# Recurrence gates as four 64x64 tiles, recurrence products moved off GpSimd, and the next layer's modulation moved into the recurrence's stage

## The chip, the cores and the metric

The kernel runs on one core of one Trainium2 chip. The metric is the device time of one execution in microseconds; the times of the kernel before are the median of three runs. In the profile PE is the matrix engine, PEld its weight loads, DVE the vector engine, ACT the scalar engine, POOL is GpSimd, and SP is the queue from which every DMA of this kernel is issued.

## The reference, cut to what matters

The program is a trunk of two layers over 512 latent and 256 context tokens of width 1024. Each layer normalises the tokens, scales and shifts them by a modulation that is computed from the conditioning vectors, multiplies them by one wide input projection, and feeds three branches: a gated delta rule (GDN), a gated linear recurrence (RG-LRU) and neighbourhood attention. Each branch has a SiLU gate path and a branch projection, the three are merged under sigmoid gates, and one output projection with a modulated residual ends the layer.

```python
shift, scale, gate = split(silu(c) @ w_mod[l] + b_mod[l], 3)      # also for c_ctx
h = rms_norm(x, g_pre[l]) * (1 + scale) + shift

def rglru(x, wa, ba, wx, bx, lam, h0):       # one direction; two are run
    r = sigmoid(block_diag_linear(x, wa, ba))     # 8 blocks of 64 x 64
    i = sigmoid(block_diag_linear(x, wx, bx))
    a = exp(-8 * r * softplus(-lam))
    b = sqrt(1 - a * a) * (i * x)
    h[t] = a[t] * h[t - 1] + b[t]
merged = g0 * (ya @ w_branch[0]) + g1 * (yb @ w_branch[1]) + g2 * (yc @ w_branch[2])
x = x + gate * rms_norm(merged @ w_out, g_post[l])
```

The second layer has no context output, so most of its work covers only the 512 latent tokens.

## The kernel before

Every fp32 matrix is split into two fp16 parts (`whi`, `wlo`), and a projection is three fp16 products: high by high, high by the low part of the data, low by high. Weights come from HBM in raw tiles of 512 KB (256 KB for a branch projection) through a ring of three slots (`raw_t`, L305); ACT makes the high part, DVE the low part.

The order of the instructions is written by a planner (`Flow`, L50). Generators ask it for times (`fl.until`), it keeps estimated clocks for every engine, and it emits the instructions in the order of its own clock; each engine then runs them strictly in that order. A layer's main generator walks through `schedule(l)` (L208): the GDN and attention inputs; the first merge stage `gb(2)` (eight pairs of a gate projection `g` and a branch projection `b` for attention), beside which the second half of the GDN's chunk chain still runs; the projections `za`; the recurrence's stage with the tokens zb 0, xb 0, xb 1, zb 1, xb 2, zb 2, xb 3, zb 3; then `gb(0)` for the GDN branch, two `g` and two `b` of branch 1, the token `out`, the rest of `gb(1)` and the output projection. The first branch-1 projection waits until all recurrence groups have ended (`yield core`, L1653).

**The recurrence** (`rg_core`, L886) works on four groups of 128 channels, each with two of the 64-wide blocks. Per group: the convolution; `xh` and `xl`, the fp16 parts of its result; the weights `lw`, for each direction and gate a 128x128 matrix with two 64x64 blocks on the diagonal and zeros beside them; then `yield before` (L899), which holds the group until the group before it has written its output. For each direction and each of the two gates (`tr`, `ti`) there are two segments (512 and 256 columns) of three products into one PSUM bank, evacuated by ACT with a tanh. ACT computes `aa` and the second tanh, DVE squares `aa`, ACT takes the square root of `zz`, GpSimd multiplies `ix` by `zz` (L934), DVE runs four scans, GpSimd adds the two directions (L953), DVE multiplies by the SiLU gate and ACT and DVE write the fp16 output `yb`.

**The modulation** of the next layer (`modulation`, L519; `mod_rows`, L475) is computed in two halves of eight steps. A step takes a 512 KB tile `wm` and issues eight products `pm` of 128x32 tiles in four column strips. After the eighth, ACT copies the row out of PSUM and eight small products `pmt` turn it into columns. In layer 0 the main generator takes one step of it at each token of `gb(2)`, through `wload` (L534) and the ring of raw slots, one tile ahead; what is left is drained when `gb(2)` ends (L1658). The third part of the modulation, the gate row (`gate_rows`, L540), has its own two `wm` buffers in the recurrence's pool, is taken step by step in the recurrence's stage and `gb(0)`, and ends with a row addition on DVE, loads of `selg` and `gp` through the ring, and the broadcast products `pg`:

```python
V.tensor_tensor(row, pm, row, OP.add)
selg = raw_t([P, 2, 2, P], "selg")
nc.sync.dma_start(selg, A["selg"])
yield
for n in range(2):
    for s in range(1 if l == DEPTH - 1 else 2):
        mm(pg, selg[:, n, s, :], row, start=True, stop=True)
```

Of the kernel before, what the change touches and what calls it, by code (L numbers as in the profile page):

```python
# [14 lines left out]
OP = mybir.AluOpType  # L15
# [220 lines left out]
def build(tc, A, out):  # L236
# [282 lines left out]
    def modulation(l, out_, halves, load, rowt):  # L519

        def fin(hf):
            def f(pm):
                row = rowt()
                S.activation(row, pm, AF.Copy)
                fl.drop(pm)
                yield
                mod_cols(l, out_, row, 4 * hf, 4)
            return f

        mod_tiles(l, out_)  # L530
        for hf in halves:
            yield from mod_rows(l, hf, fin(hf), load)

    def wload(l, part, k):  # L534
        raw = raw_t([P, 2, 2, 256], "wm")
        nc.sync.dma_start(raw, A["w_mod"][l, part, k])
        fl.fetched(raw, True)
        return raw

    def gate_rows(l, pp, wp_, out_, rowt):  # L540

        row = rowt()
        nc.sync.dma_start(row, A["b_gate"][l])

        def fin(pm):
            V.tensor_tensor(row, pm, row, OP.add)
            fl.drop(pm)
            gg = pp.tile([P, 2, D], F32, name="gg")
            selg = raw_t([P, 2, 2, P], "selg")
            nc.sync.dma_start(selg, A["selg"])  # L550
            fl.fetched(selg, True)
            g = A["g_post"]
            gp = raw_t([P, D], "gp")
            nc.sync.dma_start(gp, bass.AP(tensor=g.tensor, offset=g.offset + l * D, ap=[[0, P], [1, D]]))
            fl.fetched(gp, True)
# [3 lines that stand above are left out]
                    pg = pst(f"pg{l}_{n}_{s}", [P, 512])  # L559
                    mm(pg, selg[:, n, s, :], row, start=True, stop=True)  # L560
                    V.scalar_tensor_tensor(gg[:, s, n * 512:(n + 1) * 512], pg, 1.0 / SW,
                                           gp[:, n * 512:(n + 1) * 512], op0=OP.mult, op1=OP.mult)
            fl.drop(selg, gp)
            fl.used[selg.name] = fl.now
            out_["gg"] = gg

        def load(l, part, i):
            t = wp_.tile([P, 2, 2, 256], F32, tag="wm", name="wm", bufs=2)
            nc.sync.dma_start(t, A["w_mod"][l, part, i])
            fl.fetched(t)  # L570
            return t

        yield from mod_rows(l, 2, fin, load, 2)
# [189 lines left out]
    def layer(l, mod, first):  # L763
# [116 lines left out]
        def load_lw(j):  # L880
            t = rp.tile([P, 4, P], F32, tag="lw", name="lw", bufs=2)
            nc.sync.dma_start(t, A["lru_w"][l, j])
            fl.fetched(t)
            return t

        def rg_core(pp, yb, j, lwr, b, before):  # L886
# [5 lines left out]
            yield fl.until(xh)  # L892
            V.tensor_tensor(xl, xb[:, :NT + GAP], xh, OP.subtract)
            yield fl.until(lwr)
            lw = [pp.tile([P, 4, P], F16, tag=f"lw{i}", name=f"lw{i}", bufs=2) for i in range(2)]
            S.activation(lw[0], lwr, AF.Copy, scale=SW)
            yield fl.until(lw[0])
            V.scalar_tensor_tensor(lw[1], lwr, SW, lw[0], op0=OP.mult, op1=OP.subtract)
            yield before  # L899
            yield fl.until(xl, *lw)  # L900
            aa = pp.tile([P, 2, NT], F32, tag="aa", name="aa")
# [3 lines left out]
            for d in range(2):  # L905
                tr = pp.tile([P, NT], F32, tag="tr", name="tr")
                ti = pp.tile([P, NT], F32, tag="ti", name="ti")
                for w_, dst in ((0, tr), (1, ti)):
                    wi = (d * 2 + w_) * 4 + j
                    for a, b, xo in xsegs:  # L910
                        yield from fl.room()
                        p = pst("lru", [P, b - a])
                        for n, (i, x_) in enumerate(((0, xh), (0, xl), (1, xh))):
                            mm(p, lw[i][:, d * 2 + w_, :], x_[:, xo:xo + b - a], start=n == 0, stop=n == 2)
                        S.activation(dst[:, a:b], p, AF.Tanh, scale=0.5 / SW, bias=lrb[:, wi:wi + 1])
                        yield 0.0
                if d == 1:
# [9 lines left out]
                yield fl.until(aa)  # L927
                V.tensor_tensor(zz[:, d, :], aa[:, d, :], aa[:, d, :], OP.mult)
                yield fl.until(tr, zz)
# [3 lines left out]
            yield fl.until(zz)  # L933
            G.tensor_tensor(ix, ix, zz, OP.mult)  # L934
            yield fl.until(ix)
            hs = []
            for d in range(2):
                hh = pp.tile([P, NT], F32, tag=("tr", "ti")[d], name="hh")
                if d == 0:
# [9 lines left out]
                hs.append(hh)  # L949
                yield fl.until(hh)  # L950
            z = zview(yb, j)
            yield lambda: ("zb", j) in gates and gates["zb", j].done
            G.tensor_tensor(hs[0][:, :ntok], hs[0][:, :ntok], hs[1][:, :ntok], OP.add)  # L953
            yield fl.until(hs[0])
            V.tensor_tensor(hs[0][:, :ntok], hs[0][:, :ntok], z[:, :ntok], OP.mult)
            yield fl.until(hs[0])
            yield from put_y(yb, j, hs[0], 0.5 * UN)
            yield fl.until(yb)

        xfree = []  # L960
        BLK = (0, 8, 24, 32)
# [639 lines left out]

        merged, gated = {}, {}
        nxt, read, turned = {}, set(), []
        with ExitStack() as layer_:
# [11 lines left out]
            for tkn in schedule(l):  # L1616
                kind = tkn[0]
                if kind == "merge":
# [6 lines left out]
                    for half in halves:  # L1625
                        for u in range(2):
                            outs.append(fl.spawn(gdn_out(mp, half, ya, u, ended(*outs)), 4))
                    side = iter(()) if last else modulation(l + 1, nxt, (0, 1), wload, rowt)
                    continue
# [34 lines left out]
                if kind == "xb" and tkn[1]:  # L1664
                    lwr = load_lw(tkn[1])
                if kind in ("xb", "zb") and rp is not None:
                    if need is not None:
                        yield fl.until(need)
                    need = next(side, None)
# [5 lines left out]
                if opening and kind == "xb":  # L1675
# [7 lines left out]
                    rp = rgs.enter_context(tc.tile_pool(name=f"rg{l}", bufs=1, side="right", reuse_waits="tile"))  # L1683
                    side = gate_rows(l, ggp, rp, nxt, rowt)
                if kind == "a":
# [115 lines left out]
def _layout(i):  # L1801
# [27 lines left out]
    o["lru_b"] = np.stack([a["lru_ba"], a["lru_bx"]], 2).reshape(L, 16, P).transpose(0, 2, 1)  # L1829
    lw = np.zeros((L, P, 2, 2, 4, P), np.float32)  # L1830
    for k, name in enumerate(("lru_wa", "lru_wx")):
        v = a[name].reshape(L, 2, 4, 2, 64, 64)
        for b in range(2):
            lw[:, 64 * b:64 * b + 64, :, k, :, 64 * b:64 * b + 64] = v[:, :, :, b].transpose(0, 3, 1, 2, 4)
    o["lru_w"] = lw.reshape(L, P, 4, 4, P).transpose(0, 3, 1, 2, 4)
    pool = np.concatenate([a["rpb"].reshape(L, NH, -1), np.full((L, NH, 1), NEG, np.float32),
# [34 lines left out]
```

## Time and profile before

| what | value |
|---|---|
| time, median of 3 runs | 1683.18 us (1683.06 to 1683.78) |
| the profiled execution's own time | 1683.76 us |
| its span, first to last instruction | 1682.0 us |
| mean granted clock of the matrix engine | 0.993 |
| busy: PE, DVE, ACT, GpSimd | 1616.8, 1206.9, 877.9, 279.5 us |

A busy PE counts from a product's start to its modelled end, and products overlap: one of 512 fp16 columns is shown with 379 ns although the next starts long before that. So two products' starts tell the cost, not their durations. Layer 0's first merge stage lies from 417 to about 608 us, its recurrence's stage from 608 to 692, `gb(0)` to 807; in layer 1 the recurrence's stage begins at about 1427 and `gb(0)` ends at about 1577.

### The profile page before, as it was taken

To read this page: it belongs to the slowest core of one execution; us is meant where nothing else is said; L and a number is where in the kernel's file an instruction comes from. 1 tells how busy PE (TensorE), PEld (TensorE's weight loads), DVE (VectorE), ACT (ScalarE), POOL (GpSimd) and SP (SyncE) were. 2 spreads that over 40 slices of the span, in tenths; PEclk is the share of its full clock that TensorE was granted. 3 is DMA by queue.
4 is the path that set the end of the run, shared out by engine and by line. 5 is a ranking of instruction groups with operands and counts; after the bars stand their busy time and mean duration, and the time that the engine had idled before them with its cause. 6 is when DMAs were issued, how large, how long until landed. Compare 5 with 4: busy or idle time off the path is not lost. (4 is left out here: it accounts for less than half of the span.)

```text
span 1682.0 us, 30788 instructions
## 1 busy us (share of the span) xinstructions
PE 1616.8 (96%) x11652; PEld 1027.5 (61%) x11652; DVE 1206.9 (72%) x2896; ACT 877.9 (52%) x2107; POOL 279.5 (17%) x423
## 2 busy tenths in 40 slices
PE   5999999999999999999999999999999999999997
PEld 3666877766667655565664565677766666544443
DVE  5678888775878737775445666989777998688654
ACT  4446665545555426662344544766455666656531
POOL 3003120001322001132120001222003220013310
PEclk9999999999999999999999999999999999999999
DMA  9211011121222333223242122110121112532432
GB/s 369 68 63 58 27 45 45 39 65 36 89 70 70 107 120 125 75 65 101 87 158 80 60 64 64 57 33 28 56 70 50 57 39 76 170 113 88 142 122 76
DMA packets 48389, 139.83 MB, mean 83 GB/s; under 512 B 8048, under 2 KB 8688, under 8 KB 48240
## 3 DMA queue, kind: packets, MB, share of 16 engines
q1 hardware_dynamic: 48240, 137.86, 25.4%
q8 instruction: 91, 1.49, 0.4%
q14 instruction: 58, 0.48, 0.1%
HBM read 133.64 MB, written 4.19 MB: 82 GB/s over the span
## 5 line engine op out<-in xcount | busy, mean ns | idle before, releaser
L264 PEld LDWEIGHTS <-whi_g 128*128 128x128 f16 x1152 | 108.3, 98 | 77.3 <-issue 1.2
L199 DVE SCALAR_TENSOR_TENSOR wlo_g<-raw,whi_g 128x512 f16<-128x512 f32 x96 | 90.7, 985 | 23.8 <-ACT whi_g L199 23.8
L264 PE MATMUL py<-wo,mg 128*128 128x512 f16 x480 | 104.7, 379 | 1.5 <-ACT mt L199 1.5
L264 PEld LDWEIGHTS <-whi_a 128*128 128x128 f16 x736 | 69.1, 98 | 46.2 <-issue 2.7
L264 PE MATMUL 1_g<-h,whi_g 128*128 128x512 f16 x384 | 93.7, 379 | 0.0
L199 ACT ACTIVATE X<-px 128x256 f16<-128x256 f32 x169 | 63.0, 383 | 58.2 <-PE px L264 54.7
L264 PE MATMUL 0_g<-h,whi_g 128*128 128x512 f16 x384 | 93.1, 379 | 0.0
L199 DVE SCALAR_TENSOR_TENSOR coa<-cba,cva,coa 128x770 f32<-128x770 f32 (+1 forms) x72 | 70.8, 984 | 17.2 <-ACT coa L199 15.9
L264 PEld LDWEIGHTS <-mg 128*128 128x128 f16 x480 | 47.0, 98 | 57.2 <-issue 1.8
L199 ACT ACTIVATE di<-py 64x128 f16<-64x128 f32 x234 | 62.8, 271 | 33.5 <-PE py L264 14.2
L264 PEld LDWEIGHTS <-whi_b 128*128 128x128 f16 x576 | 53.5, 98 | 41.0 <-issue 3.4
L199 POOL TENSOR_SCALAR_AFFINE_SELECT dec<-dec 128x256 f32<-128x256 f32 x48 | 23.6, 498 | 325.6 <-ACT dec L199 284.5
L264 PEld LDWEIGHTS <-wlo_g 128*128 128x128 f16 x576 | 54.3, 98 | 37.0
L199 POOL MEMSET cba<- 128x2 f32 (+1 forms) x72 | 3.8, 100 | 436.9 <-DVE coa L199 304.4
L199 DVE TENSOR_TENSOR ic<-pp,lmc 128x128 f16<-128x128 f32 x240 | 65.3, 284 | 4.0 <-PE pp L264 1.1
L199 ACT ACTIVATE whi_g<-raw 128x512 f16<-128x512 f32 x96 | 55.1, 626 | 13.3 <-DMA raw<-in_w_in 13.2
L199 POOL TENSOR_TENSOR gm<-trir,gst 128x256 fp32r<-128x256 f32 x96 | 61.6, 667 | 1.2
L264 PEld LDWEIGHTS <-di 128*128 128x128 f16 x480 | 41.2, 98 | 31.0 <-issue 9.6
L199 DVE CAST di<-py 64x128 f16<-64x128 f32 x150 | 43.0, 287 | 23.9 <-ACT di L199 15.9
L199 DVE SCALAR_TENSOR_TENSOR wlo_b<-raw,whi_b 128x512 f16<-128x512 f32 x48 | 38.6, 804 | 21.4 <-ACT whi_b L199 21.4
L264 PE MATMUL pp<-X,ld 128*128 128x64 f16 x480 | 51.8, 192 | 2.3 <-ACT Y L199 0.3
L199 POOL TENSOR_TENSOR mt<-mg,mt 128x768 f32<-128x768 f32 (+1 forms) x16 | 33.1, 2072 | 117.6 <-DVE mt L199 117.6
(657 smaller groups left out, 4401.6 us busy)
## 6 DMA issues: line engine op xcount, KB each, us to landing
raw<-in_w_in SPq DMA_DIRECT2D x128, 512.0 KB, 3.6
wm<-in_w_mod SPq DMA_DIRECT2D x48, 512.0 KB, 4.3
raw<-in_w_branch SPq DMA_DIRECT2D x48, 256.0 KB, 2.6
rwo<-in_w_out SPq DMA_DIRECT2D x16, 512.0 KB, 3.6
xt<-in_xin SPq DMA_DIRECT2D x12, 512.0 KB, 5.0
bias<-in_rpb SPq DMA_DIRECT2D x24, 256.0 KB, 2.9
lw<-in_lru_w SPq DMA_DIRECT2D x8, 256.0 KB, 3.4
x<-xo SPq DMA_DIRECT2D x4, 512.0 KB, 2.9
```

What stands on the lines that cost most here:

```text
L199: return real(*args, **kw)
L264: nc.tensor.matmul(dst, lhsT, rhs, **kw)
```

## The change

- **Gates.** `lw` holds, per direction, four 64x64 blocks: rows 0 to 63 the first gate's, rows 64 to 127 the second gate's, columns by block. Each of the three terms is four products of 64x64 tiles at tile positions (0,0), (0,64), (64,0), (64,64), which write both gates' banks, a bank each. Since each gate needs both blocks in its own row half, `xh` and `xl` get copies with the halves exchanged (`xs0`, `xs1`), made by four DMAs on SP per group. Two banks are asked for at once (`fl.room(2)`).
- **Groups overlap.** Instead of the group before having ended, a group's gates wait for its scans (`scanned`); `tr` and `ti` have two buffers; the wait for the group before stands at the end.
- **Engines.** The square of `aa` goes from DVE to ACT; the product `ix` by `zz` (in two halves) and the sum of the directions go from GpSimd to DVE.
- **Modulation.** `modulation(l + 1)` runs behind the gate row's steps (`aside`), with the gate row's `wm` buffers, two tiles ahead. Steps are taken at the tokens of the recurrence's stage, in layer 0 two per token from zb 1 on (before and after its projection), none at xb 1, and at the tokens of `gb(0)`. The first merge stage has none.

```diff
-    def wload(l, part, k):
-        raw = raw_t([P, 2, 2, 256], "wm")
...
+            yield from mod_rows(l, hf, fin(hf), load, 2)
+    def wload_of(wp_):
+        def load(l, part, i):
+            t = wp_.tile([P, 2, 2, 256], F32, tag="wm", name="wm", bufs=2)
+            nc.sync.dma_start(t, A["w_mod"][l, part, i])
+            fl.fetched(t)
+            return t
+        return load
...
             V.tensor_tensor(xl, xb[:, :NT + GAP], xh, OP.subtract)
+            yield fl.until(xl)
+            xsw = []
+            for i, x_ in enumerate((xh, xl)):
+                xsw.append(pp.tile([P, NT + GAP], F16, tag=f"xs{i}", name=f"xs{i}"))
+                for a in (0, 64):
+                    nc.sync.dma_start(xsw[i][a:a + 64], x_[64 - a:128 - a])
+                fl.ready[xsw[i].name] = fl.now + FETCH + 0.5
...
-            yield before
-            yield fl.until(xl, *lw)
+            yield lambda: len(scanned) >= j
+            yield fl.until(xl, *xsw, *lw)
...
-                for w_, dst in ((0, tr), (1, ti)):
-                    wi = (d * 2 + w_) * 4 + j
-                    for a, b, xo in xsegs:
-                        yield from fl.room()
-                        p = pst("lru", [P, b - a])
-                        for n, (i, x_) in enumerate(((0, xh), (0, xl), (1, xh))):
-                            mm(p, lw[i][:, d * 2 + w_, :], x_[:, xo:xo + b - a], start=n == 0, stop=n == 2)
-                        S.activation(dst[:, a:b], p, AF.Tanh, scale=0.5 / SW, bias=lrb[:, wi:wi + 1])
-                        yield 0.0
+                for a, b, xo in xsegs:
+                    yield from fl.room(2)
+                    ps = [pst(f"lru{w_}", [P, b - a]) for w_ in range(2)]
+                    cols = slice(xo, xo + b - a)
+                    for n, (i, x_) in enumerate(((0, 0), (0, 1), (1, 0))):
+                        for w_, h0 in ((0, 0), (0, 1), (1, 0), (1, 1)):
+                            r_, c_ = slice(64 * w_, 64 * w_ + 64), slice(64 * h0, 64 * h0 + 64)
+                            nc.tensor.matmul(ps[w_][c_], lw[i][r_, d, c_], ((xh, xl) if h0 == w_ else xsw)[x_][r_, cols],
+                                             start=n == 0, stop=n == 2, tile_position=(64 * w_, 64 * h0))
+                        fl.product(ps[0], (b - a) / 2400.0 + 0.03)
+                    fl.product(ps[1], 0.0)
+                    for w_, dst in ((0, tr), (1, ti)):
+                        wi = (d * 2 + w_) * 4 + j
+                        S.activation(dst[:, a:b], ps[w_], AF.Tanh, scale=0.5 / SW, bias=lrb[:, wi:wi + 1])
+                    yield 0.0
...
-                V.tensor_tensor(zz[:, d, :], aa[:, d, :], aa[:, d, :], OP.mult)
+                S.activation(zz[:, d, :], aa[:, d, :], AF.Square)
...
-            G.tensor_tensor(ix, ix, zz, OP.mult)
-            yield fl.until(ix)
             hs = []
             for d in range(2):
-                hh = pp.tile([P, NT], F32, tag=("tr", "ti")[d], name="hh")
+                V.tensor_tensor(ix[:, d], ix[:, d], zz[:, d], OP.mult)
+                yield fl.until(ix)
+                hh = pp.tile([P, NT], F32, tag=("tr", "ti")[d], name="hh", bufs=2)
...
+            scanned.append(j)
...
-            G.tensor_tensor(hs[0][:, :ntok], hs[0][:, :ntok], hs[1][:, :ntok], OP.add)
+            V.tensor_tensor(hs[0][:, :ntok], hs[0][:, :ntok], hs[1][:, :ntok], OP.add)
...
+            yield before
...
+        def aside(load):
+            yield from gate_rows(l, ggp, load, nxt, rowt)
+            if not last:
+                yield from modulation(l + 1, nxt, (0, 1), load, rowt)
...
-                    side = iter(()) if last else modulation(l + 1, nxt, (0, 1), wload, rowt)
+                    side = iter(())
...
-                if kind in ("xb", "zb") and rp is not None:
+                if kind in ("xb", "zb") and rp is not None and tkn != ("xb", 1):
                     if need is not None:
                         yield fl.until(need)
                     need = next(side, None)
...
-                    side = gate_rows(l, ggp, rp, nxt, rowt)
+                    side = aside(wload_of(rp))
+                    need = next(side)
+                if not last and kind in ("xb", "zb") and rp is not None and tkn not in (("xb", 0), ("xb", 1)):
+                    if need is not None:
+                        yield fl.until(need)
+                    need = next(side, None)
```

The layout function builds `lru_w` for the new tiles. Blank lines are left out.

## Rows read from the trace of the kernel before

**Rows 1.** The page, part 1: an engine's busy time, share and instructions

```profile
PE 1616.8 (96%) x11652; PEld 1027.5 (61%) x11652; DVE 1206.9 (72%) x2896; ACT 877.9 (52%) x2107; POOL 279.5 (17%) x423
```

**Rows 2.** Stages: length, then busy PE PEld DVE ACT POOL, PEclk, DMA share, GB/s

```profile
417.00:608.00 191.00, 184.25 (x1626) 127.63 (x1625) 141.63 (x407) 93.63 (x270) 33.23 (x59) 0.98 0.27 83
608.00:692.00 84.00, 84.00 (x546) 49.07 (x544) 53.03 (x64) 49.98 (x72) 9.11 (x12) 1.00 0.37 123
1492.00:1577.00 85.00, 83.72 (x408) 38.55 (x406) 69.33 (x79) 53.01 (x79) 27.51 (x14) 1.00 0.29 90
```

**Rows 3.** PE's waits, 1430 to 1682 us: total, times, longest

```profile
PE pg L264 <- ACT whi_b L199: 1.3, 1, 1.3
PE b L264 <- ACT yb L199: 0.9, 1, 0.9
PE b L264 <- DVE yb L199: 0.4, 1, 0.4
```

**Rows 4.** Tile lru, its products: duration in ns, min/median/max

```profile
L264 PE MATMUL lru<-xh,lw x128: 271/326/379, 636.7 to 1554.9; 128*128 128x512 f16 x64, 128*128 128x256 f16 x64
L264 PE MATMUL lru<-xl,lw x64: 272/326/379, 637.0 to 1554.8; 128*128 128x512 f16 x32, 128*128 128x256 f16 x32
```

**Rows 5.** Timeline of PE, 644.6 to 648.4 us: start, length to the last end

```profile
644.76 0.38 PE L264 MATMUL lru<-xh,lw 128*128 128x512 f16 x1
644.98 0.38 PE L264 MATMUL lru<-xl,lw 128*128 128x512 f16 x1
...
646.71 0.82 PE L264 MATMUL 0_zb_1c<-h,wlo_zb 128*128 128x256 f16 x6
647.46 0.64 PE L488 MATMUL pm<-wm,sc 128*32 128x256 f32 x8
648.03 0.60 PE L264 MATMUL 0_xb<-h,whi_xb 128*128 128x512 f16 x2
```

**Rows 6.** Timeline of PE, 586.4 to 594.2 us; idle time before it, releaser in brackets

```profile
586.47 0.64 PE L488 MATMUL pm<-wm,sc 128*32 128x256 f32 x8
589.74 1.08 PE L488 MATMUL pm<-wm,sc 128*32 128x256 f32 x8 [2.63 <-DMA wm<-in_w_mod]
591.53 1.87 PE L264 MATMUL pmt<-sel,row 128*128 128x4 f32 x8 [0.71 <-ACT row L199]
```

**Rows 7.** Stages, end of layer 0's first merge stage

```profile
586.00:593.00 7.00, 3.66 (x28) 2.07 (x27) 1.02 (x2) 1.54 (x2) 0.00 (x0) 0.74 0.64 198
593.00:597.00 4.00, 4.00 (x13) 1.66 (x14) 1.73 (x5) 0.00 (x0) 0.00 (x0) 0.60 0.28 80
```

**Rows 8.** Timeline of DVE, 1500 to 1551 us

```profile
1500.99 0.68 DVE L199 TENSOR_TENSOR row<-pm,row 128x512 f32<-128x512 f32 x1
1501.60 2.99 DVE L199 SCALAR_TENSOR_TENSOR wlo_b<-raw,whi_b 128x512 f16<-128x512 f32 x1
...
1543.76 2.11 DVE L199 TENSOR_TENSOR_SCAN hh<-aa,hh,ix 128x512 f32<-128x512 f32 x1
...
1550.03 0.68 DVE L199 SCALAR_TENSOR_TENSOR wlo_b<-raw,whi_b 128x512 f16<-128x512 f32 x1
```

**Rows 9.** Tile selg: its DMA issue (ns) and landing (us)

```profile
L550 SPq DMA_DIRECT2D selg<-in_selg x2: 327/328/328, 693.8 to 1504.6; - x2
...
DMA to landing us min/median/max: 2.5/2.6/2.7
```

**Rows 10.** Groups by shape, whole span: busy us, mean ns, idle before

```profile
L199 POOL TENSOR_TENSOR ix<-ix,zz 128x1536 f32<-128x1536 f32 x8 | 27.6, 3452 | 117.7 <-ACT zz L199 117.7
...
L264 PEld LDWEIGHTS <-lw 128*128 128x128 f16 x192 | 18.7, 98 | 15.6 <-issue 0.6
...
L199 DVE TENSOR_TENSOR zz<-aa 128x768 f32<-128x768 f32 x16 | 15.3, 957 | 2.8 <-ACT aa L199 2.8
```

**Rows 11.** Timeline of ACT, 1518 to 1552 us

```profile
1518.72 1.03 ACT L199 ACTIVATE tr<-lru,lrb 128x512 f32<-128x512 f32 x2
...
1550.21 1.05 ACT L199 ACTIVATE tr<-lru,lrb 128x512 f32<-128x512 f32 x2 [0.30 <-DVE yb L199]
```

More of the change, by code (lines that the diff above doesn't have):

```diff
@@ L531, in modulation, with gate_rows @@
         for hf in halves:
-            yield from mod_rows(l, hf, fin(hf), load)
-    def wload(l, part, k):
-        raw = raw_t([P, 2, 2, 256], "wm")
[L536 to L540, printed above, removed]
+            yield from mod_rows(l, hf, fin(hf), load, 2)
[6 more added lines that the diff above has]
+        return load
+    def gate_rows(l, pp, load, out_, rowt):
         row = rowt()
@@ L565, in fin @@
             out_["gg"] = gg
[L567 to L571, printed above, removed]
         yield from mod_rows(l, 2, fin, load, 2)
@@ L880, in load_lw @@
         def load_lw(j):
-            t = rp.tile([P, 4, P], F32, tag="lw", name="lw", bufs=2)
+            t = rp.tile([P, 2, P], F32, tag="lw", name="lw", bufs=2)
             nc.sync.dma_start(t, A["lru_w"][l, j])
@@ L893, in rg_core @@
             V.tensor_tensor(xl, xb[:, :NT + GAP], xh, OP.subtract)
+            yield fl.until(xl)
[5 more added lines that the diff above has]
+                fl.ready[xsw[i].name] = fl.now + FETCH + 0.5
             yield fl.until(lwr)
-            lw = [pp.tile([P, 4, P], F16, tag=f"lw{i}", name=f"lw{i}", bufs=2) for i in range(2)]
+            lw = [pp.tile([P, 2, P], F16, tag=f"lw{i}", name=f"lw{i}", bufs=2) for i in range(2)]
             S.activation(lw[0], lwr, AF.Copy, scale=SW)
@@ L905, in rg_core @@
             for d in range(2):
-                tr = pp.tile([P, NT], F32, tag="tr", name="tr")
-                ti = pp.tile([P, NT], F32, tag="ti", name="ti")
-                for w_, dst in ((0, tr), (1, ti)):
-                    wi = (d * 2 + w_) * 4 + j
-                    for a, b, xo in xsegs:
-                        yield from fl.room()
-                        p = pst("lru", [P, b - a])
-                        for n, (i, x_) in enumerate(((0, xh), (0, xl), (1, xh))):
-                            mm(p, lw[i][:, d * 2 + w_, :], x_[:, xo:xo + b - a], start=n == 0, stop=n == 2)
-                        S.activation(dst[:, a:b], p, AF.Tanh, scale=0.5 / SW, bias=lrb[:, wi:wi + 1])
-                        yield 0.0
+                tr = pp.tile([P, NT], F32, tag="tr", name="tr", bufs=2)
+                ti = pp.tile([P, NT], F32, tag="ti", name="ti", bufs=2)
+                for a, b, xo in xsegs:
[13 more added lines that the diff above has]
+                    yield 0.0
                 if d == 1:
@@ L958, in rg_core @@
             yield fl.until(yb)
-        xfree = []
+            yield before
+        xfree, scanned = [], []
         BLK = (0, 8, 24, 32)
@@ L1829, in _layout @@
     o["lru_b"] = np.stack([a["lru_ba"], a["lru_bx"]], 2).reshape(L, 16, P).transpose(0, 2, 1)
-    lw = np.zeros((L, P, 2, 2, 4, P), np.float32)
+    lw = np.zeros((L, 4, P, 2, P), np.float32)
     for k, name in enumerate(("lru_wa", "lru_wx")):
@@ L1833, in _layout @@
         for b in range(2):
-            lw[:, 64 * b:64 * b + 64, :, k, :, 64 * b:64 * b + 64] = v[:, :, :, b].transpose(0, 3, 1, 2, 4)
-    o["lru_w"] = lw.reshape(L, P, 4, 4, P).transpose(0, 3, 1, 2, 4)
+            lw[:, :, 64 * k:64 * k + 64, :, 64 * b:64 * b + 64] = v[:, :, :, b].transpose(0, 2, 3, 1, 4)
+    o["lru_w"] = lw
     pool = np.concatenate([a["rpb"].reshape(L, NH, -1), np.full((L, NH, 1), NEG, np.float32),
```

## The prediction

> **What bounds the kernel now.** The page first [rows 1]: PE is busy for 96% of the span, so the question is which stage it really fills. The view by stages answers it [rows 2]: in layer 0's recurrence stage (608 to 692) PE is busy for all 84 us, in layer 1's (1492 to 1577) for 83.72 of 85, while in layer 0's first merge stage (417 to 608) 6.75 of 191 us are empty and the granted clock is 0.98 on average. The list of PE's waits from 1430 on [rows 3] shows where layer 1 loses time: 1.3 us at the gate row's broadcast (pg), 0.9 and 0.4 at the first branch-1 product, for the recurrence's output yb. So PE is the bound where the change works: product time taken out there shortens the run, unless the recurrence, which ends in layer 1 just when PE asks for it, holds PE instead.
>
> **The gate products.** Now each of the 8 groups (4 per layer) issues 24 products, 192 in all, half of 512 columns and half of 256 [rows 4]. In the timeline [rows 5] two 512-column ones start 0.22 us apart (644.76, 644.98); six of 256 columns take 0.82 us, 0.27 of it the last one's length [rows 4]: (0.82 - 0.27)/5 = 0.11. So 96 x 0.22 + 96 x 0.11 = 31.7 us of PE. Afterwards there are 48 products per group, in fours, each four covering both gates for one of three terms: 48 fours of 512 columns and 48 of 256. What a four of tiles costs the trace shows only for four column strips of 32: the eight modulation products pm at 647.46 take 0.64 us to the end of the last. That one alone is as long as a plain one of its stream or longer (over 0.27), so the second four started at most 0.37 us after the first, where eight products in turn would start seven streams apart. The strips run side by side. I take 0.02 us over one stream for a four of 64x64 tiles: 48 x 0.24 + 48 x 0.13 = 17.8 us. Entering and leaving the tiled form costs too [rows 5]: 647.46 is 0.2 us after the last plain product started (646.71 + 5 x 0.11 = 647.26) instead of 0.11, and I put the exit at the same 0.09: 0.2 us a burst. With 16 bursts (both segments of a direction together) 3.2 us, with 32 (each alone) 6.4. Together 21.0 to 24.2, a gain of 7.5 to 10.7; I take **-9**. That two row halves overlap as column strips do is not in the trace; the bounds are one stream for a four (-10.7) and four streams for a four (the slower rival).
>
> A rule speaks against this. In the trace the first products of both pm fours use all rows, and 0.64 us for eight leaves no room for weight loads in the open between them. The Trainium skill, TensorE: Matmul & The Clock Gate, Part 3 (Measured speedup vs the span model), says weight loads overlap running matmuls only where the row group differs; here each four meets the row groups of the four before. By it the fours would pay their loads openly, as in the third rival; so far the pm rows speak against it.
>
> **The modulation moves.** Sixteen steps of eight products, 0.57 us each (647.46 to 648.03), leave layer 0's first merge stage and come back in its recurrence stage and the gb(0) products behind it, both full: nothing won, nothing lost. What goes is the drain at the stage's end [rows 6, 7]. There the last steps stand alone: PE waits 2.63 us for a weight tile and 0.71 for row, 3.34 empty of the 7 us from 586, and the clock falls: 0.74 and 0.60 granted in the two stretches. 4 us at 0.60 is 3.2 us at the lower level (1.2 GHz), in which 1.6 us of work is lost: 3.3 + 1.6 = 4.9, **-5**. In the new place tiles are fetched two steps ahead; by my count 11 of the 27 steps are taken before gb(0) and 16 in it, so only the eight pmt products remain for the end, with row ready. Neighbouring steps share an entry and exit: **-1** (0 to -2). The cost is in the count as well: layer 0's gate row ends its last step behind xb 3 and its broadcast opens zb 3, with no projection between. There PE waits for the DVE's row addition, between 0.68 (DVE free) and 3.7 (a split of 2.99 in front of it) [rows 8]: nearer to the free one, **+1.5**. In layer 1 a longer g projection now lies between the two, which covers the 1.3 us [rows 3]: **-1.3**.
>
> SP's queue takes the 16 loads of 512 KB on other ring slots, and 32 new swaps (4 per group, 96 KB) between them. A 256 KB load landed 2.6 us after issue and an issue takes 0.33 [rows 9]; the planner reckons 2.5 for all four, so PE may stand 1 to 2 us at a first group's gates; later groups' swaps are out long before the scans that gate them. Bounds 0 to 4 over two layers: **+1**. A weight load queued behind a swap waits no longer than xl is late.
>
> **The recurrence's engines.** GpSimd loses 8 products of 3.45 us [rows 10] and 8 sums. DVE takes two halves of about 0.96 us and a sum of at most that per group and gives two squares of 0.957 to ACT [rows 10]: up to +1 us a group. In return GpSimd no longer works beside it: a wlo_b split took 2.99 us in that stretch, 0.68 elsewhere [rows 8]. So DVE stays near its 69.33 of 85 us [rows 2], and ACT (53.01 there) has room for 8 us of squares. On the path: layer 1's groups follow each other by 31.5 us (gates evacuated at 1518.72 and 1550.21 [rows 11]), since a group waits for its predecessor's last output. When it waits for the scans instead, the stretch from the scan's end (1543.76 + 2.11 [rows 8]) to 1550.21 is gone, 4.3 us, and 1.5 more as 3.45 becomes 2 x 0.96. Three intervals give 17 us. PE asks for yb only 7 us sooner than now (half of 9, 1.3 for pg, 1.3 for yb itself), so that wait ends: **-1.3**. Layer 0 has no such wait, and 9 us of modulation is added in front of it: nothing. The next to be late would be yb again, once PE gained 17 us more.
>
> **The sum.** -9 - 5 - 1 + 1.5 - 1.3 + 1 - 1.3 = -15.1. The profiled execution took 1683.76 us (span 1682.0 and 1.76 around it): 1668.7. The median of the runs lies 0.6 lower, so 1668.
>
> **Rivals.** *The row halves take turns.* For: no row of the trace has two row tiles. Then a four costs two streams, 31.7 as now, plus 4.8 of switching: -15.1 + 9 + 4.8 = -1.3, about 1682. *Holes*: the moved modulation filled holes beside layer 0's delta-rule chain, and taking it out shortens that stage by the drain alone, 16 x 0.57 = 9 us less gain: 1677. For: 3.4 of the empty 6.75 us lie elsewhere in that stage. Against: the projections za 2, za 3, zb 0 and xb 0 stand behind as filler. *Weight loads in the open*: 96 fours pay 0.098 us each (a weight load's length [rows 10]): +9.4, 1678. By that page's rule this is what happens. *Slower*: the four tiles run one after another. Then the products cost twice 31.7, with 4.8 of switching 36.5 more than now instead of 9 less: 1668.7 + 45.5, about 1714. It decides from the point where it eats the other terms' 6.1: a mean four of 0.34 us ((31.7 + 6.1 - 4.8)/96) against my 0.185. Against it: the eight pm in 0.64 us. That the diff doesn't do what it says I see no room for: the 64x64 weights and the swapped copies are laid out for it.
>
> **How the numbers follow.** My forecast has 0.73 (1668, give or take 8: the bounds of gates, broadcast and swaps, and 3 us for an emitted order that changes everywhere). Row halves in turns 0.08, holes 0.08, open weight loads 0.05, slower 0.06. The range 1660 to 1680 holds the forecast and the two rivals at 1677 and 1678; it leaves out the serial one, most of the turns and the forecast's tails, some 0.2. A measurement here tells about 0.2%, 3.4 us, from no change, so faster means under 1679.8: the forecast, most of holes and loads, 0.83. Same: the turns and the edge of those two, 0.09. Slower: the serial tiles and a rest, 0.08.
>
> **What the changed profile would show.** Right: 384 lru products, in bursts of twelve whose fours start 0.22 to 0.24 us apart; no wait for wm near the end of the first merge stage, and the clock there at 1.00; no PE wait for yb in layer 1; no ix on GpSimd. A wait of 1 to 2 us at pg in layer 0 would confirm that term. Wrong: fours 0.43 us apart or more; PE empty at the gates for the swaps; layer 0's time from the first merge to xb 0 shorter by less than 10 us; DVE's splits late, with PE waiting for a wlo.

## The result, and the profile after

| what | before | after |
|---|---|---|
| time, median of 4 runs each | 1683.12 us (1681.32 to 1683.78) | 1661.17 us (1659.61 to 1662.66) |
| ratio, 95% interval | | 0.9873 (0.9858 to 0.9887) |
| the profiled execution's own time and span | 1683.76, 1682.0 us | 1660.49, 1658.8 us |
| mean granted clock | 0.993 | 0.996 |

The change makes the kernel 1.3% faster. The forecast of 1668 lay 7 us above it, with 1660 as its lower end. The page's first part answers to [rows 1]: PE is still busy for 96% of a shorter span, GpSimd's busy time is down from 279.5 to 235.3 us, and DVE, which took over that work, is busy for 12.8 us less than before.

```profile
PE 1599.4 (96%) x11844; PEld 1015.0 (61%) x11844; DVE 1194.1 (72%) x2905; ACT 887.5 (54%) x2122; POOL 235.3 (14%) x407
```

To see where the time went, take tiles that PE reaches in both kernels at the same point of the program, and compare when they start. These are their product groups before: after the durations (min/median/max in ns) stand the first and the last start in us, and the last line is the same tile from 1400 us on, layer 1.

```profile
L264 PE MATMUL 0_xb<-h,whi_xb x64: 379/379/389, 619.4 to 668.2; 128*128 128x512 f16 x64
...
L264 PE MATMUL 1_xb<-h,whi_xb x64: 378/379/390, 1433.1 to 1476.7; 128*128 128x512 f16 x64
...
L264 PE MATMUL b<-yb,whi_b x128: 376/379/389, 807.6 to 1629.1; 128*128 128x512 f16 x128
...
L264 PE MATMUL b<-yb,whi_b x64: 376/379/389, 1576.6 to 1629.1; 128*128 128x512 f16 x64
```

And after:

```profile
L264 PE MATMUL 0_xb<-h,whi_xb x64: 379/379/390, 600.1 to 650.0; 128*128 128x512 f16 x64
...
L264 PE MATMUL 1_xb<-h,whi_xb x64: 379/379/389, 1419.8 to 1462.4; 128*128 128x512 f16 x64
...
L264 PE MATMUL b<-yb,whi_b x128: 379/379/379, 795.0 to 1607.0; 128*128 128x512 f16 x128
...
L264 PE MATMUL b<-yb,whi_b x64: 379/379/379, 1556.3 to 1607.0; 128*128 128x512 f16 x64
```

Read as a ledger: at xb 0 of layer 0 the new kernel is 19.3 us ahead (619.4 to 600.1). At the first branch-1 product of that layer only 12.6 are left, because the moved modulation is paid there. At xb 0 of layer 1 it is 13.3 ahead, at that layer's first branch-1 product 20.3, at the last of them 22.1, and at the end 23.2. So layer 1, which has no modulation to move, gained about 9 us between its xb 0 and its last branch-1 product.

The stages show the same; the columns are those of [rows 2]. Layer 0's first merge stage lost part of its empty time (4 of 172 us are empty where 6.75 of 191 were) and runs at a granted clock of 1.00 instead of 0.98. In layer 1 PE is no longer empty at all, GpSimd's 27.51 us of 85 have become 11.76 of 81, and DVE is at 65.37.

```profile
417.00:589.00 172.00, 167.98 (x1484) 122.57 (x1482) 140.76 (x400) 93.03 (x267) 33.79 (x59) 1.00 0.15 45
589.00:675.00 86.00, 85.14 (x625) 48.28 (x624) 57.48 (x74) 52.44 (x76) 0.48 (x9) 1.00 0.50 162
1476.00:1557.00 81.00, 81.00 (x475) 36.11 (x474) 65.37 (x87) 58.87 (x90) 11.76 (x8) 1.00 0.38 119
```

PE's waits answer to [rows 3]. From 600 to 800 us the first line below is the only one, from 1410 to the end the second: the waits for yb and for the gate row in layer 1 are gone, and a wait of 0.9 us at pg has appeared in layer 0. The third line is from the kernel before, 1400 to 1682 us: there py, the output projection at the tail, waited 1.5 us for the merged sum mt. In this run and those below that wait is between 0.3 and 1.5, whatever the edit.

```profile
PE pg L264 <- ACT tr L199: 0.9, 1, 0.9
...
PE py L264 <- ACT mt L199: 0.3, 1, 0.3
...
PE py L264 <- ACT mt L199: 1.5, 1, 1.5
```

Now the gates themselves. Tile lru had 192 products of full size [rows 4]; it has 384 of a quarter each:

```profile
L920 PE MATMUL lru<-xs,lw x192: 267/333/401, 620.1 to 1531.9; 64*64 64x512 f16 x96, 64*64 64x256 f16 x96
L920 PE MATMUL lru<-xh,lw x128: 267/335/401, 620.1 to 1531.9; 64*64 64x512 f16 x64, 64*64 64x256 f16 x64
L920 PE MATMUL lru<-xl,lw x64: 269/322/400, 620.4 to 1531.8; 64*64 64x512 f16 x32, 64*64 64x256 f16 x32
```

PE's timeline shows one burst, 24 products between two plain ones:

```profile
619.84 0.38 PE L264 MATMUL 0_zb<-h,wlo_zb 128*128 128x512 f16 x1
620.15 0.40 PE L920 MATMUL lru<-xh,lw 64*64 64x512 f16 x1
620.15 0.40 PE L920 MATMUL lru<-xs,lw 64*64 64x512 f16 x2
620.16 0.40 PE L920 MATMUL lru<-xh,lw 64*64 64x512 f16 x1
620.39 0.38 PE L920 MATMUL lru<-xl,lw 64*64 64x512 f16 x1
...
620.60 0.38 PE L920 MATMUL lru<-xh,lw 64*64 64x512 f16 x1
...
620.82 0.27 PE L920 MATMUL lru<-xs,lw 64*64 64x256 f16 x2
...
620.93 0.27 PE L920 MATMUL lru<-xl,lw 64*64 64x256 f16 x1
...
621.04 0.27 PE L920 MATMUL lru<-xh,lw 64*64 64x256 f16 x1
...
621.25 1.04 PE L264 MATMUL 0_zb<-h,wlo_zb 128*128 128x512 f16 x4
```

The four products of a term start within 0.01 us of each other. The next four follow after 0.24, 0.21 and 0.22 us at 512 columns and after 0.11 at 256, which is what one plain product costs [rows 5]: a four costs one stream, the first four of a burst some 0.02 more. The price is at the edges. The last plain product starts at 619.84 and would have been followed at 620.06; the burst starts 0.09 later. The last four starts at 621.04 and would have been followed at 621.15; the next plain product comes 0.10 later. So the burst takes 621.25 - 620.06 = 1.19 us, where the twelve products that it replaces took 646.71 - 644.76 = 1.95 [rows 5]: 0.76 us saved.

Two of the sixteen bursts are not like that. One, at 678.66 and 681.05 in layer 0, is split by other products, so that it enters and leaves the tiled form twice and takes 1.42. The other is the first of layer 1:

```profile
1441.93 0.40 PE L920 MATMUL lru<-xh,lw 64*64 64x512 f16 x1
...
1442.17 0.38 PE L920 MATMUL lru<-xl,lw 64*64 64x512 f16 x1
1442.32 0.79 PE L920 MATMUL lru<-xs,lw 64*64 64x512 f16 x2
1442.74 0.40 PE L920 MATMUL lru<-xl,lw 64*64 64x512 f16 x1
...
1443.62 1.68 PE L264 MATMUL 1_xb<-h,whi_xb 128*128 128x512 f16 x7
```

It takes 1.69 us from its first product to the next plain one, where the burst above takes 1.10. The chain of what released what shows why: the last swapped copy of xl is on its way until 1442.69, and sixteen products follow it.

```profile
1438.31 4.38 DMA xs<-xl
...
1442.74 0.95 PE lru L920 x16
```

The list of waits doesn't have these 0.6 us, because the product before is still shown as busy. Over all bursts, each from the product before it to the product behind it, PE's starts give 16 x 1.95 = 31.2 us before and 15 x 1.20 + 1.42 + 0.6 = 20.0 after. The tiles save 11.8 us, and 0.6 of that goes to a swap that lands late.

PE's weight loads in the same stretch:

```profile
619.62 0.10 PEld L264 LDWEIGHTS <-wlo_zb 128*128 128x128 f16 x1
620.14 0.90 PEld L920 LDWEIGHTS <-lw 64*64 64x64 f16 x24 [0.42 <-issue]
```

They lie in one stretch of 0.90 us, under products that use the same row halves all along, and the fours still follow each other at one stream. The Trainium skill, TensorE: Matmul & The Clock Gate, Part 3 (The mechanism), says weight loads overlap running products only where the row group differs (the prediction names the section after it for this sentence); this burst doesn't bear that out. The section after it (Measured speedup vs the span model) of that page of the Trainium skill counts about 4 ns for every further tile, with which the 0.01 us for a four agrees.

### The profile page after: what moved, and what is told of

Read it like the earlier page. It is cut to its first block, busy times and chain, and to the rows that moved or that the text cites. A ratio compares the mean times of both kernels' runs of the same rounds, so it can differ in the third digit from the quotient of the medians.

```text
span 1658.8 us, 31213 instructions
## 1 busy us (share of the span) xinstructions
PE 1599.4 (96%) x11844; PEld 1015.0 (61%) x11844; DVE 1194.1 (72%) x2905; ACT 887.5 (54%) x2122; POOL 235.3 (14%) x407
## 5 line engine op out<-in xcount | busy, mean ns | idle before, releaser
L199 DVE SCALAR_TENSOR_TENSOR wlo_g<-raw,whi_g 128x512 f16<-128x512 f32 x96 | 78.1, 854 | 20.0 <-ACT whi_g L199 20.0
L199 ACT ACTIVATE di<-py 64x128 f16<-64x128 f32 x230 | 61.8, 271 | 33.2 <-PE py L264 12.3
L199 POOL TENSOR_SCALAR_AFFINE_SELECT dec<-dec 128x256 f32<-128x256 f32 x48 | 23.2, 489 | 322.6 <-ACT dec L199 286.4
L199 POOL TENSOR_TENSOR mg<-mg,mt 128x768 f32<-128x768 f32 (+1 forms) x16 | 29.6, 1849 | 240.6 <-DVE mt L199 178.3
L199 ACT ACTIVATE whi_g<-raw 128x512 f16<-128x512 f32 x96 | 55.0, 624 | 13.3 <-DMA raw<-in_w_in 13.2
L199 DVE SCALAR_TENSOR_TENSOR wlo_b<-raw,whi_b 128x512 f16<-128x512 f32 x48 | 35.8, 746 | 31.5 <-ACT whi_b L199 31.4
```

The source lines that it names most:

```text
L199: return real(*args, **kw)
```

## Experiments

In all of them the ratio is to the kernel before, run on the same chip, with its 95% interval.

### The modulation: what of its move has a value

**The move alone**, on the kernel before (the core of the diff):

```diff
+            yield from gate_rows(l, ggp, load, nxt, rowt)
+            if not last:
+                yield from modulation(l + 1, nxt, (0, 1), load, rowt)
...
-                    side = iter(()) if last else modulation(l + 1, nxt, (0, 1), wload, rowt)
+                    side = iter(())
```

> The kernel before with the modulation's move alone (plain gates, groups one behind the other, GpSimd kept). Theory (the drain at the end of layer 0's first merge stage was waiting and a low clock, the rest of the steps only changes place): layer 0 gains 5 to 7 us, layer 1 nothing (its pg wait turns into a longer wait for yb): 1676 to 1678. Rival (holes: the steps had filled idle time and now cost their full time): 1683 or above. Rival (the move carries most of the gain): 1670 or less.

Measured 1677.12 us, 0.9966 (0.9954 to 0.9978). xb 0 of layer 0 starts at 598.9 instead of 619.4, yb's first product at 799.5 instead of 807.6: 20.5 us gained, 12.4 given back.

**The drain alone.** The modulation stays in the first merge stage of the kernel before, but what is left of it at the end is taken one step at a time at za 2, za 3 and zb 0:

```diff
-                if kind in "gb":
+                if kind in "gb" or kind == "za" or kind == "zb" and rp is None:
...
-                    if m == KD - 1:
+                    if m == KD - 1 and br != 2:
```

> The kernel before, where the modulation stays in layer 0's first merge stage and only its last steps are no longer drained at the stage's end: they are taken one by one ahead of za 2, za 3 and zb 0. Theory (what the move wins is the drain: 3.3 us empty and 1.6 us of low clock, and nothing for the place itself): about 5 us less, 1677 to 1679, with no low clock near 590. Rival (the place matters, steps beside the delta-rule chain cost more than their products): 1681 or more, though the drain is gone. Rival (it was the drain alone and more): 1675 or less.

Measured 1677.91, 0.9971 (0.9958 to 0.9983), with xb 0 at 613.1, 6.3 us earlier. The two stretches of [rows 7], where 3.34 us were empty and the clock was 0.74 and 0.60, are now these:

```profile
586.00:593.00 7.00, 7.00 (x45) 3.45 (x44) 2.15 (x3) 1.06 (x1) 0.00 (x0) 1.00 0.73 226
593.00:597.00 4.00, 4.00 (x37) 2.78 (x35) 1.11 (x2) 2.08 (x4) 0.00 (x0) 1.00 0.16 23
```

Two lines bring what the whole move brings. That was then asked of the full change: **the changed kernel with the modulation left where it was**, drained (first), or spread by the edit above (second). The core of the diff:

```diff
-                    side = iter(())
+                    side = iter(()) if last else modulation(l + 1, nxt, (0, 1), wload, rowt)
...
-                    side = aside(wload_of(rp))
-                    need = next(side)
+                    side = gate_rows(l, ggp, rp, nxt, rowt)
```

> The changed kernel with the modulation left where it was (first merge stage of layer 0, drained at its end; the gate row's steps as before): tiles, overlapping groups and engines alone. Theory (the move is worth the drain alone: 2.4 to 2.6 us of wait for wm, 0.7 for row and some 2 us at the low clock, 5 to 6 in all, less the wait at pg that it brings in layer 0): 1665 to 1668, with the waits for wm and row near 575 and a granted clock under 0.8 there. Rival (in the full kernel the sixteen steps fill holes of the recurrence's stage, so that the move is worth their 9 us too): 1671 to 1675. Second rival (the move is worth nothing once the groups overlap): 1661 to 1663.

> As e10_no_move, but the last modulation steps are taken at za 2, za 3 and zb 0 instead of drained at the end of the stage (the edit of e8_drain_spread). Theory (nothing of the move but the drain has a value, and the moved form pays for a wait at pg of layer 0 and for a longer stage there): 1660 to 1663, as the changed kernel, with no wait for wm and the clock at 1.00 after 586. Rival (also the neighbouring steps' shared switching, 1 to 2 us, and the cover of pg in layer 1, 1.3 us, belong to the move): 1663 to 1665. Second rival (the move costs more than it brings, and this beats the changed kernel as e6_spaced does): 1656 to 1659.

Measured 1669.20, 0.9920 (0.9906 to 0.9934), and 1661.56, 0.9872 (0.9858 to 0.9887). The second is the changed kernel's time. PE's timeline of the first has the waits of [rows 6] again, and its clock is 0.77 and 0.55 in the two stretches:

```profile
589.73 1.08 PE L488 MATMUL pm<-wm,sc 128*32 128x256 f32 x8 [2.50 <-DMA wm<-in_w_mod]
591.52 1.87 PE L264 MATMUL pmt<-sel,row 128*128 128x4 f32 x8 [0.72 <-ACT row L199]
```

From the first to the second, xb 0 goes from 619.6 to 613.0 (6.6 us) and keeps that lead to the end. Against the changed kernel, the second is 12.9 us behind at xb 0 (613.0 to 600.1) and 0.4 behind at yb (795.4 to 795.0): the steps cost nearly as much in the one place as in the other, although in the new one PE also waits 0.9 us at pg. The first came out a little above its expected 1665 to 1668: the drain is worth 7.6 us between these medians, of which 6.6 are at the drain and 0.9 at the tail (py waits 1.5 us for mt in the one, 0.6 in the other).

### The gates: the tiles alone, and without them

**Tiles and swaps alone**, on the kernel before (the core of the diff), and the **changed kernel with plain 128x128 gates**, which undoes it there:

```diff
-                        for n, (i, x_) in enumerate(((0, xh), (0, xl), (1, xh))):
-                            mm(p, lw[i][:, d * 2 + w_, :], x_[:, xo:xo + b - a], start=n == 0, stop=n == 2)
+                    for n, (i, x_) in enumerate(((0, 0), (0, 1), (1, 0))):
+                        for w_, h0 in ((0, 0), (0, 1), (1, 0), (1, 1)):
+                            r_, c_ = slice(64 * w_, 64 * w_ + 64), slice(64 * h0, 64 * h0 + 64)
+                            nc.tensor.matmul(ps[w_][c_], lw[i][r_, d, c_], ((xh, xl) if h0 == w_ else xsw)[x_][r_, cols],
+                                             start=n == 0, stop=n == 2, tile_position=(64 * w_, 64 * h0))
```

> The kernel before with the 64x64 gate tiles and their swaps alone; groups stay one behind the other, the modulation and GpSimd's work stay. Theory (the matrix engine bounds, the recurrence of layer 1 ends just in time): a burst of 24 small products now costs 1.2 us where 12 plain ones cost 1.95, so 16 bursts free 12 us; layer 0's 6 us show, layer 1's are mostly lost in a longer wait for yb, whose groups still follow each other by about 31 us: 1675 to 1678, with 4 to 6 us of waiting for yb in layer 1. Rival (the tiles carry the whole gain by themselves): 1671 or less and no longer wait for yb. Rival (tiles are worth nothing without the rest): 1683.

> The changed kernel with plain 128x128 gate products and no swaps. Theory (tiles are worth 12 us of the matrix engine in both layers, now that no recurrence waits): 1672 to 1674, and no wait for yb. Rival (the gain of the tiles is covered by something else, such as the recurrence): 1661 to 1664.

Measured 1679.32, 0.9979 (0.9970 to 0.9988), and 1674.70, 0.9951 (0.9939 to 0.9963). Added to the kernel before, the tiles bring 0.2%; taken out of the changed kernel, they cost 0.8% (0.9951 against 0.9873), 13.5 us between the medians and 12.3 between the profiled spans. Of the latter 1.4 are a longer wait at pg in layer 0 (2.3 instead of 0.9). Without that wait, layer 0 from xb 0 to yb takes 5.9 us longer (202.2 and 194.9 with it) and the way on to layer 1's yb 5.6 (766.9 and 761.3): 11.5 us for the tiles and their swaps, close to the 11.2 counted burst by burst. Both times came out slower than expected, 1679.32 above 1675 to 1678 and 1674.70 just above 1672 to 1674. The waits of the tiles alone, layer 1 from 1425 us on, say why:

```profile
PE b L264 <- ACT yb L199: 7.8, 1, 7.8
PE py L264 <- ACT mt L199: 1.5, 1, 1.5
PE b L264 <- ACT tr L199: 0.4, 1, 0.4
PE lru L922 <- DMA xs<-xl: 0.2, 1, 0.2
```

PE comes to the first branch-1 product at 1563.3 instead of 1576.6, 13.3 us sooner, and then stands there for yb, 7.8 us where 4 to 6 were expected. At the last branch-1 product only 3.7 us of the lead are left (1629.1 to 1625.4). The recurrence didn't get faster, only PE did. The last line is the visible part of what the swaps cost here: that burst, again the first of layer 1, takes 2.07 us from its first product to the next plain one (1448.18 to 1450.25), 1.0 more than a burst that waits for nothing.

### The recurrence: overlap and engines

**Groups held until the one before has ended**, and **the product and the sum left on GpSimd**, each an undoing in the changed kernel:

```diff
-            yield lambda: len(scanned) >= j
+            yield before
```

```diff
+            G.tensor_tensor(ix, ix, zz, OP.mult)
+            yield fl.until(ix)
...
-                V.tensor_tensor(ix[:, d], ix[:, d], zz[:, d], OP.mult)
-                yield fl.until(ix)
...
-            V.tensor_tensor(hs[0][:, :ntok], hs[0][:, :ntok], hs[1][:, :ntok], OP.add)
+            G.tensor_tensor(hs[0][:, :ntok], hs[0][:, :ntok], hs[1][:, :ntok], OP.add)
```

> The changed kernel with each group held until the group before has ended (as before), all else kept. Theory (layer 1's yb is on the edge, 1.6 us early): its four groups then follow each other by about 31 us instead of 27, yb comes some 12 us later and the matrix engine waits about 10: 1670 to 1673, layer 0 unchanged. Rival (the engines' move off GpSimd alone shortens the groups enough, or other work hides the wait): 1661 to 1664.

> The changed kernel with the recurrence's product and sum left on GpSimd, groups overlapping, tiles and modulation as changed. Theory (the engines' move shortens layer 1's groups, whose last output is only 1.6 us early): per group 1.5 us for the product (3.45 instead of two of 0.96) and about 1 us for the sum, and DVE slower beside GpSimd; four groups make 6 to 12 us, less 1.6 of margin: a wait for yb of 4 to 10 us and 1665 to 1671. Rival (overlapping alone is enough, the engine does not matter): 1660 to 1663.

Measured 1673.54, 0.9945 (0.9932 to 0.9957), and 1669.56, 0.9925 (0.9911 to 0.9939). Layer 0 has no wait for yb in either. In layer 1, from 1425 us on, the first has

```profile
PE b L264 <- ACT yb L199: 10.3, 1, 10.3
PE py L264 <- ACT mt L199: 0.7, 1, 0.7
```

and the second

```profile
PE b L264 <- ACT yb L199: 5.2, 1, 5.2
PE py L264 <- ACT mt L199: 0.8, 1, 0.8
```

Waits of this length cost more than themselves, for the clock is low behind them. In the first of the two:

```profile
1567.00:1571.00 4.00, 3.49 (x8) 1.09 (x8) 2.41 (x4) 1.87 (x4) 0.00 (x0) 0.50 0.38 125
```

From the first to the last branch-1 product of layer 1 PE takes 50.7 us in the changed kernel (1556.3 to 1607.0), 63.4 with the groups held (1555.6 to 1619.0) and 59.0 with GpSimd kept (1559.2 to 1618.2): 12.7 and 8.3 us more, 2.4 and 3.1 beyond the waits. The clock was 0.50 behind the second wait too, from 1566 to 1570. So these two stretches hold what the two undoings cost (12.4 and 8.4 us between medians); the first came out just above its expected 1670 to 1673.

The changed kernel has no such wait, but little in hand. ACT's timeline has the gates evacuated at these times; these are the second and third group, the fourth and last follows at 1524.50, so groups are 26.7 us apart, where it was 31.5 [rows 11].

```profile
1470.99 0.69 ACT L199 ACTIVATE tr<-lru,lrb 128x512 f32<-128x512 f32 x1
...
1497.70 0.69 ACT L199 ACTIVATE tr<-lru,lrb 128x512 f32<-128x512 f32 x1 [6.18 <-PE lru L920]
```

The last output comes from DVE at 1554.02 + 0.69 = 1554.7:

```profile
1554.02 0.69 DVE L199 SCALAR_TENSOR_TENSOR yb<-hh,yb 128x512 f16<-128x512 f32 x1 [0.70 <-ACT yb L199]
```

PE starts on yb at 1556.3, and its first six products read earlier groups (in the run of the tiles alone the wait stands after six): some 3 us in hand. Overlap and engines together are what turns the tiles' gain in layer 1 into time, and neither is enough alone. Two things were not run apart: overlap and engines without tiles and move, and the square on ACT instead of DVE.

### One more step, and steps in pairs

The wait at pg in layer 0 comes from the gate row ending just before its broadcast. **One more step, behind xb 1**, ends it a token earlier:

```diff
-                if not last and kind in ("xb", "zb") and rp is not None and tkn not in (("xb", 0), ("xb", 1)):
+                if not last and kind in ("xb", "zb") and rp is not None and tkn != ("xb", 0):
```

> The changed kernel with one more modulation step behind xb 1 in layer 0, so that a projection lies between the gate row's last step and its broadcast. Theory: the wait at pg in layer 0 (0.9 us idle, 1.2 between starts) goes and nothing else changes: 1 us less, 1660. Rival (the step behind xb 1 meets its tile too early): the same or 1 to 2 us more, with a wait for wm.

Measured 1657.78 (1656.19 to 1659.30), 0.9851 (0.9838 to 0.9865). No wait is left at pg: it starts at 655.84, right behind the projection. yb's first product in layer 0 comes 1.6 us sooner (793.4). The rest of the difference lies in the next layer, and the spans of the changed kernel's own four runs lie between 1657.9 and 1660.9 us. So 1.6 us is what the profile shows for the edit; the medians' 3.4 us are more than it explains.

**Steps in pairs**, to save entries and exits of the tiled form, on top of that edit: two steps at each gate projection of layer 0's `gb(0)` but the last and none at its branch projections; then the same with the first pair left out and one step at the last branch projection.

```diff
-                if kind in "gb":
+                two = kind == "g" and tkn[1] == 0 and tkn[2] < KD - 1 and not last
+                for _ in range(2 if two else 0 if kind == "b" and tkn[1] == 0 and not last else kind in "gb"):
```

```diff
-                if kind in "gb":
+                n_ = int(kind in "gb")
+                if n_ and tkn[1] == 0 and not last:
+                    n_ = (2 if tkn[2] > 0 else 0) if kind == "g" else int(tkn[2] == KD - 1)
+                for _ in range(n_):
```

> As the spaced one, and in gb(0) of layer 0 two modulation steps at each gate projection instead of one at every token. Theory (an entry into the tiled form and the exit cost 0.2 us a burst): some seven bursts fewer save 1.4 us more, 1658 to 1659. Rival (pairs meet tiles that have not landed, or the switch is free): as the spaced one or more.

> The changed kernel with the one more step behind xb 1 (as in e6_spaced) and, in gb(0) of layer 0, two modulation steps at each gate projection from the second on, one at the last branch projection and none elsewhere; so neighbouring steps share an entry and exit of the tiled form, and no step is taken back to back with one at zb 3. Theory (e7_paired lost to a first pair whose second tile had not landed, 3.1 us empty and a fall of the clock, and the switching of tile forms is worth about 0.2 us a burst): seven bursts saved, 1.4 us below e6_spaced's 1657.8, so 1656 to 1657, no PE wait for wm. Rival (paired steps cost as much as single ones, the gain of e7 to yb of layer 0 was something else): 1657.5 to 1658.5. Second rival (two tiles at once are late each time, since the ring has two buffers): waits of PE for wm at several g, 1660 or more.

The first took 1662.92, 0.9879 (0.9865 to 0.9893), the second 1657.21 (1655.86 to 1659.45), 0.9854 (0.9840 to 0.9867). The first failed at one place, which PE's timeline shows. The last step of zb 3 and the first of the pair run together at 667.85, a burst of the gates follows, and then the pair's second step finds its tile still under way: three steps at once for two buffers. The clock in the ten us from 665 was 0.89.

```profile
667.85 1.07 PE L488 MATMUL pm<-wm,sc 128*32 128x256 f32 x16
...
673.12 1.08 PE L488 MATMUL pm<-wm,sc 128*32 128x256 f32 x8 [3.09 <-DMA wm<-in_w_mod]
```

The second has no such wait, and yb's first product comes at 792.3, 1.1 us before the single steps' (0.8 of it behind xb 0). In the time it can't be told from the single steps (ratios 0.9854 and 0.9851), so whether the pairs are worth the 1.4 us that the theory gave them stays open. Either of the two has a lower median than both kernels; its interval still touches the changed kernel's (0.9858 to 0.9887). The single steps are the simpler edit.

## Why the prediction was right, and where its sum was off

The forecast case held: PE bounds both stages, the tiles take product time out, the recurrence gets out of PE's way, and the drain goes. None of the rivals did: the fours don't take turns and don't run serially, no weight load stands in the open, and the moved steps had filled no holes (12.9 us out of one stage, 12.5 into the next). Term by term:

- **Gates, -9.** Mis-sized: -11.8 by the bursts, outside the stated 7.5 to 10.7. The term that was off is "I take 0.02 us over one stream for a four of 64x64 tiles": a four costs one stream, and only the first four of a burst 0.02 more. The bound of -10.7 that the text called one stream for a four still carried that 0.02; without it the same sum gives 48 x 0.22 + 48 x 0.11 + 3.2 = 19.0 against 31.7. The entry and exit at 0.09 each (0.09 and 0.10 here) were right, and the sixteen bursts were seventeen.
- **Drain, -5.** 6.3 in the one pair of kernels and 6.6 in the other.
- **Shared entries, -1, and the moved steps at nothing.** The changed kernel is 0.4 us ahead at yb of the one whose steps stay and are spread, with 0.9 lost at pg: 1.3. With pg's wait ended it is 2.0 ahead (793.4 to 795.4).
- **pg in layer 0, +1.5.** Right in kind: 0.9 us of wait, and the edit that ends it gives 1.6.
- **pg in layer 1, -1.3.** Right in number, not in reason. The wait is gone, but also where the modulation and the gate row's steps were left as before. It is gone with the tiles alone as well. With the move alone, the longer g projection was there, and pg waited 1.5 us for selg. So the longer projection isn't what ended it; what did stays open, and a shift of the whole stage is the likely cause.
- **Swaps, +1.** Right in kind, at the first group's gates of layer 1: 0.6 us in the changed kernel, 1.0 with the tiles alone. Layer 0's first group doesn't wait.
- **yb in layer 1, -1.3.** Gone, 1.8 us between the first and the last branch-1 product (20.3 to 22.1). Yet the margin was misjudged: "once PE gained 17 us more" leaves out the 7 us by which PE comes sooner in the same paragraph, and about 3 are in hand. Counted from xb 0 of layer 1, PE asks 7.0 us sooner than before (20.3 - 13.3), as reckoned; the last output comes 11.6 sooner (1579.6 to 1554.7, less 13.3), not 17. Groups follow at 26.7 us, not at the 25.7 reckoned, and the first one's gates start 1.7 us later behind xb 0 (22.1 instead of 20.4).

With the measured terms the sum is -11.8 + 0.6 - 6.6 - 1.3 + 0.9 - 1.3 - 1.8 = -21.3, and the tail's wait for mt, which no step foresaw, adds 1.2 (1.5 to 0.3): -22.5, where the span lost 23.2. The missing 0.7 lies between layer 0's first branch-1 product and layer 1's xb 0 (12.6 to 13.3), where nothing was edited. The forecast was 7 us too cautious, mainly at the gates, the drain and that tail, and the time lies only 1.2 us inside the range's lower end.

## What to carry to other kernels

A change of several parts is not the sum of its parts' own runs: here the tiles alone gave 0.2%, but taken out of the whole they cost 0.8%, because most of what they gain PE in layer 1 went into waiting for the recurrence until the recurrence was shortened too. So ask of every gain on the bounding engine by how much its next supplier is early, in us. Look beside the list of waits at the starts of products too: a late transfer can hide under a product that is still shown as busy. And before moving work to another stage, look for what the old place does badly: here a drain of a few steps held all the value of the move, and two lines would have had it.

## What the hardware showed that was not expected

- Four 64x64 products on the four quarters of the array cost one stream (0.21 to 0.22 us at 512 fp16 columns, 0.11 at 256; 0.24 for the first four of a burst). Changing between plain and tiled form costs 0.09 on the way in and 0.10 on the way out.
- DVE beside GpSimd. With the product left on GpSimd (3.43 us, the first line below, with another of GpSimd's operations of 1.72 us right behind it), two `wlo_g` splits took 5.24 us in that stretch. In the changed kernel such a pair took 1.27 us at 1544.35, with nothing of GpSimd beside it. The Trainium skill, GPSIMD Engine Reference, section 1 (Specifications), says the two engines share their SBUF interfaces; how much that costs only these rows say. It is a reason why DVE isn't busier for the work that it took over: with product and sum left on GpSimd DVE is busy for 1194.8 us in all, with both on DVE for 1194.1. First GpSimd's, then DVE's timeline of the run with the product on GpSimd:

```profile
1524.79 3.43 POOL L199 TENSOR_TENSOR ix<-ix,zz 128x1536 f32<-128x1536 f32 x1 [6.70 <-ACT zz L199]
...
1525.20 5.24 DVE L199 SCALAR_TENSOR_TENSOR wlo_g<-raw,whi_g 128x512 f16<-128x512 f32 x2 [1.17 <-ACT whi_g L199]
```

- The low clock after a stretch with little work showed at two places. One is the drain, beside a wait for a weight tile: 0.74 and 0.60 [rows 7], 0.77 and 0.55 in the run with the drain kept, and 1.00 with the same steps spread; a pair that met a tile that had not landed had 0.89 over ten us. The other is the wait for yb in layer 1: behind 5.2, 7.8 and 10.3 us of it the clock was 0.50 over four us.
